# One more feed-forward tile by Strassen's scheme, and two small reorderings in the attention of a hybrid decoder block

## The chip, the cores and the metric

The kernel runs on one core of one Trainium2 chip. The metric is the device time of one execution, in microseconds (us). The engines are named as in the profile: PE multiplies matrices (PEld loads its weights), DVE and ACT work element by element, POOL and SP mostly issue transfers. Sixteen DMA engines move data.

## The reference, cut to what matters

One decoder layer on 512 tokens of width 1024. After an RMS norm, one projection feeds an attention mixer (8 heads; a compressed branch of 31 blocks, a selected and a sliding-window branch) and an RWKV-7 mixer. They are gated, merged and added to the residual. A second norm leads to the feed-forward part that most of the change is about:

```
def conv_ffn(h, w_up, conv_w, conv_b, w_down):
    u = h @ w_up
    s = u.shape[1]
    up = jnp.pad(u, ((0, 0), (CONV_WIDTH - 1, 0), (0, 0)))
    c = conv_b + conv_w[0] * up[:, 0:s]
    for j in range(1, CONV_WIDTH):
        c = c + conv_w[j] * up[:, j:j + s]
    val, gate = jnp.split(c, 2, axis=-1)
    return (jax.nn.silu(gate) * val) @ w_down
```

The other change is in the compressed branch of the attention:

```
    s_c = jnp.einsum('bgrsd,bcgd->bgrsc', q, kc).astype(jnp.float32) + bias_c
    p_c = masked_softmax(s_c, dist_c >= 0, axis=-1)
    o_cmp = jnp.einsum('bgrsc,bcgd->bsgrd', p_c, vc)
```

## The kernel before

Every large product is made of three products of 32-bit "rounded" parts: a weight tile is loaded by SP's queue into one of three `raw` buffers, ACT rounds it to `whi`, DVE subtracts to get `wlo` (L366), each with two buffers, and PE multiplies (hi, hi), (lo, hi) and (hi, lo). A load into a `raw` buffer is issued when DVE's split has read what was in it. `weight_tiles` lists all tiles in the order of use, `wload` issues a load, `wsplit` makes the parts, `wnext` hands out the next pair.

The order of the work on PE is written out by hand in the stretches named here (`manual_schedule`); the order on DVE and ACT there is a scheduler's. Four stretches matter, in order of time.

**Sums of weights in memory.** `sums_in_memory` makes, for the Strassen tiles, four sums of blocks of `w_up` in a memory array `usum` of 512 rows by 128 columns per Strassen tile. Sixteen copies and sixteen accumulating transfers, of 128 rows each, run on POOL's queue while the attention computes.

**Attention.** The loop over `units` (token tile, group, branches) takes two units at a time: `turns` transposes the weights `P` of a unit on PE (L1349), `scores` makes those of the unit two places later, `values` multiplies. Filler products (`filler`) with tiles of `w_proj_b` stand between. `compressed(qt)` is the softmax of the compressed branch for token tile `qt`: 8 products with `KC` on PE and some ten small steps on `sC`, mostly on DVE. Units 0 to 3 are token tile 3, units 4 to 7 tile 2, 8 and 9 tile 1, 10 and 11 tile 0. A unit's scores are left unscaled and their scalings (`pend`, one for a whole branch and four for rows) are run inside the next call of `scores`, spread over its groups (`ng` of them).

**Merge.** Eight tiles of `w_proj_a` (m = 0 to 7, 256 KB each), 12 products of 512 columns a tile, then `w_out`.

**Feed-forward.** 22 tiles of 128 features (f). A dense tile is 48 products of 512 columns, on two weight tiles of 512 KB. Tiles f in `SF` go by Strassen's scheme with 7 half products of 12 matmuls of 256 columns (L1613), on seven 256 KB halves, of blocks of `w_up` and of `usum`; two halves are one weight tile of the queue. Before them `up_tokens` (the generator `side`) makes sums of the activations in `Hw` and their parts `R1M2` and `R3Q`, some steps after each dense tile.

Of the kernel before, what the change touches and what calls it, by code (L numbers as in the profile page):

```python
# [22 lines left out]
KT = D // 128  # L23
DH = 64
H = 8
# [10 lines left out]
NGA = 1  # L36
NGB = 7
DECAY = math.exp(-0.5)
SF = range(4, 16)

O_Q, O_KC, O_VC, O_KS, O_VS, O_KW, O_VW, O_GATE, O_RWKV, O_GA, O_GB = (
    0, 512, 640, 768, 896, 1024, 1152, 1280, 1304, 3096, 4120)
# [42 lines left out]
def hybrid_block(ctx: ExitStack, tc: tile.TileContext, A: dict, out: bass.AP):  # L85
    nc = tc.nc
    v, sc, te = nc.vector, nc.scalar, nc.tensor
# [73 lines left out]
    for name in ("rwkv_mu", "rwkv_w0", "rwkv_a0", "rwkv_k_k", "rwkv_k_a", "rwkv_r_k", "rwkv_ln_g", "rwkv_ln_b"):  # L161
        r0, n = ROWS[name]
# [87 lines left out]
    def weight_tiles():  # L250
# [47 lines left out]
        stream = []  # L298
        for f in list(SF) + [None]:
# [8 lines left out]
                stream.append(up_block(p, 1, 1))  # L308
            if f is not None:
                stream += [up_sum(f, TS1), up_sum(f, TS3)]  # L310
        for i in range(0, len(stream) - 2, 2):
            yield stream[i:i + 2], KT, 128, v
        yield cols(A["w_up"][0], DFF + 128 * (SF[-1] + 1))
        yield stream[-2:], KT, 128, v
# [978 lines left out]
    def scores(u, n):  # L1293
        qt, g, bs = u
        qs = slice(128 * qt, 128 * qt + 128)
        N = 128 * (qt + 1)
        B = len(bs)
        P = Pb[units.index(u) % 4][:, 0:4 * B * N].rearrange("p (b r n) -> p b r n", b=B, n=N)
        nm = at.tile([128, 8], F32, name="nm", tag="nm", bufs=2)
        sm = at.tile([128, 8], F32, name="sm", tag="sm", bufs=2)  # L1300
        per = 512 // (B * N)
        todo, pend[:] = list(pend), []
        ng = 4 // per
        for r0 in range(0, 4, per):
            sp = pa()[:, 0:per * B * N].rearrange("p (r b n) -> p r b n", r=per, b=B)
            for r in range(r0, r0 + per):
                h = 4 * g + r
                for i, K in enumerate((KH, KL)):
                    mm(sp[:, r - r0], qst[:, h, qs], K[:, bs[0]:bs[0] + B, g, 0:N], i == 0, i == 1)
            for r in range(r0, r0 + per):  # L1310
                h = 4 * g + r
                for b in range(B):
                    i = 4 * b + r
                    v.tensor_tensor_reduce(out=P[:, b, r], in0=sp[:, r - r0, b], in1=BT[:, h, 384 - 128 * qt:512],  # L1314
                                           scale=-1.0, scalar=-NEG, op0=ALU.add, op1=ALU.min, accum_out=nm[:, i:i + 1])
                    act(P[:, b, r], P[:, b, r], AF.Exp, scale=-1.0, bias=nm[:, i:i + 1], accum_out=sm[:, i:i + 1])
            ig = r0 // per
            for f in todo[len(todo) * ig // ng:len(todo) * (ig + 1) // ng]:
                f()
            filler(n * (r0 + per) // 4 - n * r0 // 4)  # L1320
            yield
        v.reciprocal(sm[:, 0:4 * B], sm[:, 0:4 * B])
        for x, b in enumerate(bs):
            tt(sm[:, 4 * x:4 * x + 4], sm[:, 4 * x:4 * x + 4], gts[:, qt, 12 * g + 1 + b:12 * g + 12:3], ALU.mult)
        def row(b, r):
            i = 4 * b + r
            if r == 3:
                act(P[:, b, r], P[:, b, r], AF.Copy, scale=sm[:, i:i + 1])
            else:
                ts(P[:, b, r], P[:, b, r], sm[:, i:i + 1], None)  # L1330

        def branch(b):
            tt(P[:, b], P[:, b], sm[:, 4 * b:4 * b + 4, None].to_broadcast([128, 4, N]), ALU.mult)

        if B > 1:
            pend.append(lambda: branch(1))
        pend.extend(lambda r=r: row(0, r) for r in range(4))
        Ps[u] = P
# [50 lines left out]
    with tc.manual_schedule(engines=KTS):  # L1389
        run(scores(units[0], 12))  # L1390
        compressed(3)
        run(scores(units[1], 16))
        for i in range(0, len(units), 2):
            if i in (4, 8, 10):
                compressed_t(units[i][0])
            for j in (i, i + 1):
                a, b = turns(units[j]), scores(units[j + 2], nfill[j]) if j + 2 < len(units) else dense_only(nfill[j])
                alive = [a, b]
                while alive:
                    for x in list(alive):  # L1400
                        if next(x, alive) is alive:
                            alive.remove(x)
                    if j == 1 and len(PTk[units[1]]) == 2:
                        compressed_t(3)
            for j in (i, i + 1):
                values(units[j])
            for j in (i, i + 1):
                output(units[j])
            if i in (0, 4, 6):
                compressed({0: 2, 4: 1, 6: 0}[i])  # L1410
        filler(100)
    dbg("oaT", oaT.bitcast(F32))

# [185 lines left out]

    wpart = []  # L1600

    def up_weight():
        if not wpart:
            hi, lo = wnext(KT, 128)
            wpart.extend((hi[:, 4 * i:4 * i + 4], lo[:, 4 * i:4 * i + 4]) for i in range(2))
        return wpart.pop(0)

    def up_product(bank_, x, first=False):

        hi, lo = up_weight()  # L1610
        for k in range(8):
            for y in x[:2 - k // 4]:
                te.matmul(bank_, lhsT=(hi, lo)[k // 4][:, k % 4], rhs=y[:, k % 4], start=first and k == 0 and y is x[0],  # L1613
                          stop=k == 7, skip_group_check=not first)
# [14 lines left out]
    def up_strassen():  # L1629
# [4 lines left out]
        for f in list(SF) + [None]:  # L1634
            if f is not None:
                B1 = mmb()[:, b0]
                up_product(B1, H[0][0], True)
                u = [us[:, 3 * (f % 2) + k] for k in range(3)]
                Cg, Cv = craw[f % 2], craw[2 + f % 2]
                act(u[0], B1)  # L1640
                B2 = pa()[:, b0]
                up_product(B2, H[0][1], True)
                tt(Cg[:, b0], u[0], B2, ALU.add)
            else:
                following = dense_fm_g(hh, hl)
                next(following)
            if prev is not None:
                f_, B1_, B5_, u_, Cg_, Cv_ = prev
                up_product(B1_, H[1][1])
                act(Cg_[:, b1], B1_)  # L1650
                cg = conv(Cg_, NF + f_, f_ % 2)
            if f is not None:
                up_product(B1, M2)
                act(u[1], B1, AF.Copy, scale=-1.0)
            if prev is not None:
                up_product(B5_, Q)
                stt(Cv_[:, b0], B5_, -1.0, u_[1])
                cv = conv(Cv_, f_, 2 + f_ % 2)
                gate_value(f_, cg, cv)
            if f is not None:  # L1660
                B5 = pb()[:, b0]
                up_product(B5, R1, True)
                up_product(B1, R3)
                act(u[2], B1, AF.Copy, scale=-1.0)
                stt(Cv[:, b1], B5, -1.0, u[2])
                prev = f, B1, B5, u, Cg, Cv
# [3 lines left out]
    for f in range(NF):  # L1670
# [15 lines left out]
        if f // 2 < PD:  # L1686
            cv = conv(dense_fm(hh, hl) if f else lead[1], f, 2 + f % 2)
            gate_value(f, cg, cv)
            for _ in range(2):
                next(side, None)  # L1690
            continue
        act(cg, cg, AF.Silu)
# [232 lines left out]
```

## Time and profile before

| | |
|---|---|
| median of 3 runs | 803.11 us (802.75 to 803.26) |
| the profiled execution | 802.89 us |
| its span, first to last instruction | 801.1 us |
| outside the span | 1.8 us |
| granted clock of PE | 1.00 |
| PE, DVE, ACT, POOL busy | 790.1, 642.1, 482.8, 92.8 us |
| moved by DMA | 126.27 MB |

Times of places in the program are us from the start of the span of the profiled execution. Busy times of matmuls overlap one another, so the cost of one in a row of equal ones is read from the distance of their starts.

### The profile page before, as it was taken

To read this page: it belongs to the slowest core of one execution; us is meant where nothing else is said; L and a number is where in the kernel's file an instruction comes from. 1 tells how busy PE (TensorE), PEld (TensorE's weight loads), DVE (VectorE), ACT (ScalarE), POOL (GpSimd) and SP (SyncE) were. 2 spreads that over 40 slices of the span, in tenths; PEclk is the share of its full clock that TensorE was granted. 3 is DMA by queue.
4 is the path that set the end of the run, shared out by engine and by line. 5 is a ranking of instruction groups with operands and counts; after the bars stand their busy time and mean duration, and the time that the engine had idled before them with its cause. 6 is when DMAs were issued, how large, how long until landed. Compare 5 with 4: busy or idle time off the path is not lost.

```text
span 801.1 us, 14229 instructions
## 1 busy us (share of the span) xinstructions
PE 790.1 (99%) x5439; PEld 668.5 (83%) x5439; DVE 642.1 (80%) x1179; ACT 482.8 (60%) x929; POOL 92.8 (12%) x125
## 2 busy tenths in 40 slices
PE   7999999999999999999999999999999999999998
PEld 6788888887777887877788888999999888888886
DVE  4688899974565679888585489688898999989997
ACT  6777765454455678787344366677777754553452
POOL 5300021142000052221000000000000000002101
PEclk9999999999999999999999999999999999999999
DMA  7432323337362389999957134566666422584654
GB/s 221 125 90 68 99 74 105 86 101 210 80 132 54 79 227 271 261 261 269 196 183 243 50 133 118 154 185 182 173 184 182 128 79 80 181 309 167 234 179 153
DMA packets 138185, 126.27 MB, mean 158 GB/s; under 512 B 5806, under 2 KB 116069, under 8 KB 137989
## 3 DMA queue, kind: packets, MB, share of 16 engines
q1 hardware_dynamic: 123744, 83.21, 36.1%
q0 software_dynamic: 13312, 39.61, 18.5%
q10 hardware_dynamic: 1060, 2.55, 1.1%
q8 instruction: 42, 0.69, 0.4%
q14 instruction: 27, 0.21, 0.1%
HBM read 119.91 MB, written 29.56 MB: 187 GB/s over the span
## 4 chain that ended last, share of the span: by engine, by line
PE 90%; DVE 4%; DMA 4%; ACT 1%; issue 0%; POOL 0%; DVEq 0%
PE ps_mm L125 60%; PE ps_mm L1613 8%; PE ps_a L125 7%; PE ps_b L125 5%; PE ps_b L1613 4%; DMA usum<-in_w_up_dram 3%; PE ps_a L1613 2%; PE ps_b L1349 1%; DVE wlo L366 1%; PE ps_mm L1349 1%; DMA kc<-in_consts_dram 1%; DVE raw L131 0%; ACT whi L128 0%; PE ps_b L404 0%; PE ps_b L663 0%
## 5 line engine op out<-in xcount | busy, mean ns | idle before, releaser
L128 ACT ACTIVATE whi<-raw 128x1024 fp32r<-128x1024 f32 (+2 forms) x148 | 147.7, 999 | 129.9 <-PE ps_mm L125 61.0
L366 DVE TENSOR_TENSOR wlo<-raw,whi 128x1024 fp32r<-128x1024 f32 (+1 forms) x133 | 152.9, 1151 | 47.0 <-ACT whi L128 27.2
L125 PE MATMUL ps_mm<-hh,whi 128*128 128x512 f32 (+1 forms) x432 | 167.7, 391 | 0.3 <-ACT whi L128 0.2
L125 PE MATMUL ps_mm<-hl,whi 128*128 128x512 f32 (+1 forms) x432 | 160.5, 383 | 0.0
L125 PE MATMUL ps_mm<-hh,wlo 128*128 128x512 f32 (+1 forms) x432 | 107.9, 382 | 0.0
L125 PEld LDWEIGHTS ps_mm<-hh,whi 128*128 128x128 f32 x432 | 81.2, 188 | 18.4 <-issue 0.8
L125 PEld LDWEIGHTS ps_mm<-hh,wlo 128*128 128x128 f32 x432 | 81.2, 188 | 16.1 <-DVE wlo L366 0.3
L125 PEld LDWEIGHTS ps_mm<-hl,whi 128*128 128x128 f32 x432 | 79.2, 188 | 15.2 <-DVE hl L140 0.3
L1754 POOL DMA_DIRECT2D cgq<-in_w_down_dram x12 | 6.4, 535 | 290.0 <-DVE cgq L131 237.0
L128 ACT ACTIVATE P<-P,nm 128x512 f32<-128x512 f32 (+3 forms) x64 | 35.4, 555 | 4.5 <-DVE nm L1314 4.1
L131 DVE TENSOR_TENSOR cgq<-cgq 128x512 f32<-128x512 f32 (+1 forms) x49 | 32.9, 672 | 1.0 <-ACT cgq L128 0.2
L1314 DVE CUSTOM_DVE_ANT_0 P<-ps_a,AB 128x512 f32<-128x512 f32 (+3 forms) x64 | 30.1, 485 | 3.0 <-PE ps_a L125 2.9
L140 DVE SCALAR_TENSOR_TENSOR cgq<-cr,cw,cgq 128x511 f32<-128x511 f32 (+1 forms) x36 | 26.9, 748 | 4.4 <-ACT cgq L128 4.0
L140 DVE SCALAR_TENSOR_TENSOR cgq<-ps_mm,cw,cgq 128x511 f32<-128x511 f32 (+1 forms) x40 | 29.6, 746 | 1.1 <-ACT cgq L128 1.0
L1613 PE MATMUL ps_mm<-hl,whi 128*128 128x256 f32 x96 | 24.1, 283 | 0.0
L1613 PE MATMUL ps_mm<-hh,whi 128*128 128x256 f32 x96 | 24.1, 283 | 0.0
L128 ACT ACTIVATE QK<-ps_mm 128x64 f32<-128x64 f32 (+5 forms) x52 | 13.4, 303 | 15.3 <-PE ps_mm L125 15.2
L125 PE MATMUL ps_mm<-whi,hh 128*128 128x280 f32 (+2 forms) x72 | 22.4, 331 | 0.0
L128 ACT ACTIVATE ring<-cgq 128x1024 fp32r<-128x1024 f32 x12 | 12.7, 1060 | 15.8 <-DVE cgq L131 15.8
L125 PE MATMUL ps_mm<-whi,hl 128*128 128x280 f32 (+2 forms) x72 | 21.9, 323 | 0.0
L128 ACT ACTIVATE cgq<-ps_mm,cw 128x512 f32<-128x512 f32 x20 | 15.4, 776 | 8.8 <-PE ps_mm L125 8.0
L125 PE MATMUL ps_mm<-obT,whi 128*128 128x512 f32 x64 | 20.2, 397 | 0.0
(539 smaller groups left out, 1933.1 us busy)
## 6 DMA issues: line engine op xcount, KB each, us to landing
raw<-in_w_in_dram SPq DMA_DIRECT2D x38, 512.0 KB, 3.9
usum<-in_w_up_dram POOLq DMA_DIRECT2D x24, 768.0 KB, 23.6
raw<-in_w_down_dram SPq DMA_DIRECT2D x25, 512.0 KB, 4.0
raw<-usum SPq DMA_DIRECT2D x48, 256.0 KB, 3.3
raw<-in_w_up_dram SPq DMA_DIRECT2D x20, 512.0 KB, 3.8
raw<-in_w_up_dram SPq DMA_DIRECT2D x36, 256.0 KB, 3.3
usum<-usum POOLq DMA_DIRECT2D x8, 768.0 KB, 23.2
cgq<-in_w_down_dram POOLq DMA_DIRECT2D x12, 512.0 KB, 4.4
```

Source lines behind the costliest of these rows:

```text
L125: te.matmul(o, lhsT=l, rhs=r, start=start, stop=stop)
L128: sc.activation(o, i, f, **kw)
L131: v.tensor_tensor(o, a, b, op=op)
L140: v.scalar_tensor_tensor(o, a, s, b, op0=op0, op1=op1)
L366: eng.tensor_tensor(lo, raw, hi.bitcast(F32), op=ALU.subtract)
L1314: v.tensor_tensor_reduce(out=P[:, b, r], in0=sp[:, r - r0, b], in1=BT[:, h, 384 - 128 * qt:512], scale=-1.0, scalar=-NEG, op0=ALU.add, op1 ...
L1349: te.transpose(pt[:, 128 * i:128 * i + 128], P[:, x, i, 128 * k:128 * k + 128], ident)
L1613: te.matmul(bank_, lhsT=(hi, lo)[k // 4][:, k % 4], rhs=y[:, k % 4], start=first and k == 0 and y is x[0], stop=k == 7, skip_group_check=n ...
L1754: nc.gpsimd.dma_start(raws[g][i], A["w_down"][0][256 * g + 128 * i:256 * g + 128 * i + 128])
```

## The change

Three edits. Tile f = 3 joins the Strassen tiles, so there are 13 of them, f = 3 to 15, and three dense tiles ahead of them instead of four; `usum` grows from 1536 to 1664 columns. With 13 tiles the number of halves is odd, so the first half is a weight tile of its own, with four k-blocks. `side` takes three steps after each dense tile instead of two. In the attention, `compressed(0)` stands after the first unit of the fifth pair (j = 8) instead of after the fourth pair; and where `scores` has two groups (token tile 0), all five scalings are run after the first one.

```
-SF = range(4, 16)
+SF = range(3, 16)
...
-        for i in range(0, len(stream) - 2, 2):
+        yield stream[:1], 4, 128, v
+        for i in range(1, len(stream) - 2, 2):
             yield stream[i:i + 2], KT, 128, v
...
-            for f in todo[len(todo) * ig // ng:len(todo) * (ig + 1) // ng]:
+            for f in todo[len(todo) * ig // ng:len(todo) * (ig + 1) // ng] if ng > 2 else todo[5 * ig:5 * (ig + 1)]:
                 f()
...
+                if j == 8:
+                    compressed(0)
             for j in (i, i + 1):
                 values(units[j])
             for j in (i, i + 1):
                 output(units[j])
-            if i in (0, 4, 6):
-                compressed({0: 2, 4: 1, 6: 0}[i])
+            if i in (0, 4):
+                compressed({0: 2, 4: 1}[i])
...
-    def up_weight():
+    def up_weight(n=2):
         if not wpart:
-            hi, lo = wnext(KT, 128)
-            wpart.extend((hi[:, 4 * i:4 * i + 4], lo[:, 4 * i:4 * i + 4]) for i in range(2))
+            hi, lo = wnext(4 * n, 128)
+            wpart.extend((hi[:, 4 * i:4 * i + 4], lo[:, 4 * i:4 * i + 4]) for i in range(n))
         return wpart.pop(0)
...
-                up_product(B1, H[0][0], True)
+                up_product(B1, H[0][0], True, 1 if f == SF[0] else 2)
...
-            for _ in range(2):
+            for _ in range(3 if f < SF[0] else 2):
                 next(side, None)
```

On POOL, before, the end of the first run of sums (`usum` is the array of sums; a shape that splits a row of 128 is an accumulating transfer, the others are copies):

```order
L246 DMA usum<-in_w_up_dram 128x3x512
L243 DMA usum<-in_w_up_dram 128x1536
L246 DMA usum<-in_w_up_dram 128x3x512
L243 DMA usum<-in_w_up_dram 128x1536
L246 DMA usum<-usum 384x512
```

The same rows on POOL in the changed kernel:

```order
L246 DMA usum<-in_w_up_dram 128x4x416
L243 DMA usum<-in_w_up_dram 128x1664
L246 DMA usum<-in_w_up_dram 128x4x416
L243 DMA usum<-in_w_up_dram 128x1664
L246 DMA usum<-usum 416x512
```

The list keeps its order and its 32 transfers; each is wider by a twelfth, and those that add rows of `w_up` split a row into four pieces instead of three.

On DVE in the attention, before: the scaling of two rows of unit 9 (`P_3386`, last line) stands behind the softmax on `sC`, between the steps on the scores of unit 10 (`P_3387`).

```order
L131 TENSOR_TENSOR sC_3375<-sC_3375,kc 128x256
L366 TENSOR_TENSOR wlo<-raw,whi 128x512
L1279 TENSOR_REDUCE mx<-sC_3375 128x8
...
L1281 RECIPROCAL mx<-mx 128x8
L1314 ISA P_3387,nm<-ps_a,AB 128x128
L1314 ISA nm 128x1
L131 TENSOR_TENSOR mx<-mx,gts 128x8
L1314 ISA P_3387,nm<-ps_a,AB 128x128
L1314 ISA nm 128x1
L131 TENSOR_TENSOR sC_3375<-sC_3375,mx 128x256
L135 TENSOR_SCALAR P_3386<-P_3386,sm 128x256 x2
```

DVE at the same place in the changed kernel, from the two rows of unit 9 on:

```order
L135 TENSOR_SCALAR P_3386<-P_3386,sm 128x256 x2
L140 SCALAR_TENSOR_TENSOR AB<-AB,ps_mm 128x512
L367 TENSOR_TENSOR wlo<-raw,whi 128x512
L1315 ISA P_3387,nm<-ps_a,AB 128x128
...
L1260 COPY PTs<-ps_b 128x512
L131 TENSOR_TENSOR sC_3375<-ps_a,BC 128x256
```

The two rows are scaled ahead of the second group's scores, and the softmax begins only behind that group.

On DVE ahead of the Strassen tiles, before: `wlo_5225` and `wlo_5259` are the low parts of the last two weight tiles but two ahead of Strassen (the second of tile f = 2 and the first of f = 3), `R1M2` the low parts of summed activations.

```order
L140 SCALAR_TENSOR_TENSOR Hw_5127<-Hw_5127 128x1024
L131 TENSOR_TENSOR cgq_5120<-cgq_5120 128x512
L131 TENSOR_TENSOR R1M2_5123<-Hw_5127,R1M2_5123 128x1024
L131 TENSOR_TENSOR a2a_pairs_5128<-cgq_5120,a2a_pairs_5128 128x256
L366 TENSOR_TENSOR wlo_5225<-raw_5178,whi_5223 128x1024
L140 SCALAR_TENSOR_TENSOR cgq_5120<-ps_mm_5227,cw_72,cgq_5120 128x511
L366 TENSOR_TENSOR wlo_5259<-raw_5221,whi_5257 128x1024
```

The same place in the changed kernel: `wlo_5229` is the second weight tile of f = 2, `wlo_5264` the single half, `wlo_5310` the next two halves.

```order
L131 TENSOR_TENSOR R1M2_5123<-Hw_5127,R1M2_5123 128x1024
...
L131 TENSOR_TENSOR R1M2_5123<-Hw_5127,R1M2_5123 128x1024
L131 TENSOR_TENSOR cgq_5120<-cgq_5120 128x512
L131 TENSOR_TENSOR R3Q_5124<-Hw_5127,R3Q_5124 128x1024
L131 TENSOR_TENSOR a2a_pairs_5128<-cgq_5120,a2a_pairs_5128 128x256
L367 TENSOR_TENSOR wlo_5229<-raw_5180,whi_5227 128x1024
L140 SCALAR_TENSOR_TENSOR cgq_5120<-ps_mm_5231,cw_72,cgq_5120 128x511
L367 TENSOR_TENSOR wlo_5264<-raw_5225,whi_5262 128x512
L140 SCALAR_TENSOR_TENSOR cgq_5120<-ps_mm_5231,cw_72,cgq_5120 128x510
L131 TENSOR_TENSOR R3Q_5124<-Hw_5127,R3Q_5124 128x1024
L140 SCALAR_TENSOR_TENSOR cgq_5120<-ps_mm_5266,cw_72,cgq_5120 128x511
L367 TENSOR_TENSOR wlo_5310<-raw_5259,whi_5308 128x1024
```

Ahead of the second weight tile of f = 2 stand two more low parts of 1024 elements, one of `R1M2` and one of `R3Q`; ahead of the first whole Strassen weight tile stands the last `R3Q`.

## Rows read from the trace of the kernel before

**Rows 1.** The page, part 1: busy us (share of the span) of PE.

```profile
PE 790.1 (99%) x5439; PEld 668.5 (83%) x5439; DVE 642.1 (80%) x1179; ACT 482.8 (60%) x929; POOL 92.8 (12%) x125
```

**Rows 2.** Waits of PE: line waited for, us in total, times, longest.

```profile
PE ps_mm L1349 <- DVE P L135: 1.1, 1, 1.1
```

**Rows 3.** Windows: length, PE, PEld, DVE, ACT, POOL busy, clock, DMA share, GB/s.

```profile
482.50:493.40 10.90, 10.90 (x50) 9.03 (x49) 10.67 (x14) 7.14 (x11) 0.00 (x0) 1.00 0.32 94
```

**Rows 4.** The chain that ended last: start, us, engine, tile, line, instructions.

```profile
517.33 2.88 PE ps_b L1613 x24
...
628.64 77.76 PE ps_mm L125 x342
```

**Rows 5.** Timeline of PE in the attention: start, us, what, count, [idle before].

```profile
369.21 1.03 PE L1349 MATMUL ps_b<-kc,P 128*128 128x128 f32 x8
370.08 0.27 PE L1349 MATMUL ps_mm<-kc,P 128*128 128x128 f32 x1
371.47 0.70 PE L1349 MATMUL ps_mm<-kc,P 128*128 128x128 f32 x3 [1.12 <-DVE P L135]
371.93 0.36 PE L125 MATMUL ps_a<-KH,qst 128*128 128x256 f32 x1
```

**Rows 6.** Timeline of DVE in dense tiles f = 1 to 3.

```profile
483.47 0.75 DVE L140 SCALAR_TENSOR_TENSOR cgq<-ps_mm,cw,cgq 128x511 f32<-128x511 f32 x1 [0.23 <-ACT cgq L128]
...
489.14 1.22 DVE L366 TENSOR_TENSOR wlo<-raw,whi 128x1024 fp32r<-128x1024 f32 x1
490.27 0.74 DVE L140 SCALAR_TENSOR_TENSOR cgq<-ps_mm,cw,cgq 128x511 f32<-128x511 f32 x1
490.93 1.21 DVE L366 TENSOR_TENSOR wlo<-raw,whi 128x1024 fp32r<-128x1024 f32 x1
```

**Rows 7.** Timeline of PE at the end of tile f = 2.

```profile
491.52 1.98 PE L125 MATMUL ps_mm<-hh,wlo 128*128 128x512 f32 x8
```

**Rows 8.** Timeline of POOL: the first and the last sums.

```profile
286.28 2.11 POOL L243 DMA_DIRECT2D usum<-in_w_up_dram  x4
...
389.14 0.95 POOL L246 DMA_DIRECT2D usum<-usum  x1 [9.33 <-DMA usum<-usum]
```

**Rows 9.** DMA, 286:398: packets, MB, share; issues: KB each, median us to landing.

```profile
q0 software_dynamic: 8784, 25.30, 93.1%
...
raw<-in_w_proj_b_dram SPq DMA_DIRECT2D x7, 256.0 KB, 12.2
```

**Rows 10.** DMA, 380:385: packets, MB, share of 16 engines.

```profile
q0 software_dynamic: 423, 0.83, 89.7%
q1 hardware_dynamic: 428, 0.22, 21.6%
```

**Rows 11.** DMA issues near 389, 392, 394 and 401: last sum; w_proj_a m = 4, 5, 7.

```profile
usum<-usum POOLq DMA_DIRECT2D x1, 768.0 KB, 8.4
...
raw<-in_w_proj_a_dram SPq DMA_DIRECT2D x1, 256.0 KB, 6.0
...
raw<-in_w_proj_a_dram SPq DMA_DIRECT2D x1, 256.0 KB, 4.1
...
raw<-in_w_proj_a_dram SPq DMA_DIRECT2D x1, 256.0 KB, 2.6
```

**Rows 12.** Timeline of SP: issues of w_proj_a m = 4 and 5.

```profile
392.18 0.37 SPq L337 DMA_DIRECT2D raw<-in_w_proj_a_dram  x1
...
394.81 0.37 SPq L337 DMA_DIRECT2D raw<-in_w_proj_a_dram  x1
```

**Rows 13.** Timeline of ACT: high part of w_proj_a m = 4.

```profile
398.26 0.63 ACT L128 ACTIVATE whi<-raw 128x512 fp32r<-128x512 f32 x1 [1.98 <-DMA raw<-in_w_proj_a_dram]
```

**Rows 14.** Timeline of PE: first products of w_proj_a m = 4, 5, 6.

```profile
401.22 1.98 PE L125 MATMUL ps_mm<-oaT,whi 128*128 128x512 f32 x8
...
403.94 1.98 PE L125 MATMUL ps_mm<-oaT,whi 128*128 128x512 f32 x8
...
406.66 1.98 PE L125 MATMUL ps_mm<-oaT,whi 128*128 128x512 f32 x8
```

More of the change, by code (lines that the diff above doesn't have):

```diff
@@ L1600, in hybrid_block, with up_product @@
     wpart = []
-    def up_weight():
+    def up_weight(n=2):
         if not wpart:
-            hi, lo = wnext(KT, 128)
-            wpart.extend((hi[:, 4 * i:4 * i + 4], lo[:, 4 * i:4 * i + 4]) for i in range(2))
+            hi, lo = wnext(4 * n, 128)
+            wpart.extend((hi[:, 4 * i:4 * i + 4], lo[:, 4 * i:4 * i + 4]) for i in range(n))
         return wpart.pop(0)
-    def up_product(bank_, x, first=False):
-        hi, lo = up_weight()
+    def up_product(bank_, x, first=False, n=2):
+        hi, lo = up_weight(n)
         for k in range(8):
```

## The prediction, made before the changed kernel was run

> **What bounds the kernel now.** I read the busy times first: PE is busy 99% of the span [rows 1], so a gain must take work from PE or close one of its waits. The list of waits has little to close: apart from the start of the program, the one wait of note is 1.12 us at L1349, on a row scaling of DVE [rows 2, 5]. So I then went through the stretches that the change touches and asked how far PE's suppliers are from being late. In the dense tiles ahead of the Strassen tiles DVE is busy 10.67 of 10.90 us [rows 3]: whatever is put ahead of a weight split there makes it late. And from 286 to 398 us the sums in memory keep the DMA engines busy: POOL's queue q0 alone is 93.1% of 112 us [rows 9]. In that time a 256 KB weight tile lands 12.2 us after its issue [rows 9], against 2.6 us once the sums are over [rows 11]. The attention hides this. The merge, right behind it, takes a tile of w_proj_a every 2.72 us [rows 14], and the sums end just as it begins: the last one is issued at 389.14 and lands 8.4 us later, at 397.5 [rows 8, 11].
>
> **The tile that moves to Strassen.** A dense matmul of 512 columns costs 77.76/342 = 0.2274 us, a Strassen one of 256 columns 2.88/24 = 0.120 us [rows 4]. Dense tile: 48 x 0.2274 = 10.92. Strassen tile: 7 x 12 x 0.120 = 10.08. PE saves **0.84 us**. From the second Strassen tile on the halves pair up as before, so the steady state of that stretch should not change.
>
> **DVE ahead of the Strassen tiles.** The low part of the second weight tile of f = 2 starts at 489.14 before. The new order puts two more low parts of 1024 elements ahead of it; one such step takes 490.27 - 489.14 = 1.13 us of DVE. An idle 0.23 us at 483.47 is used up [rows 6]. So it starts at 489.14 + 2.26 - 0.23 = 491.17 and ends 1.22 us later, at 492.39. PE asks for it at 491.52 [rows 7]: **0.87 us** late. Behind it come a conv step (490.93 - 490.27 = 0.66 us [rows 6]), the half split (half of 1.13, say 0.60), a conv step, the last low part of R3Q (1.13) and a conv step: 3.71 us after 492.30, the first whole Strassen weight tile is started at 496.01 and ready at 497.23. PE, 0.87 us late, ends f = 2 eight products of 0.2274 us after 492.39, at 494.21; then come one half product (1.44) and the hi products of the next (0.96), so it asks at 496.61: another **0.62 us**. Together **1.5 us**, more than the tile saves. The rows show no spare time of DVE but the 0.23 us already used; the bounds are 0 (DVE in time after all, rival 2) and 2.2, one more conv step of 0.66 late.
>
> **The attention.** Eight transposes take 370.08 - 369.21 = 0.87 us, so the four at 370.08 need 0.43; the next group starts at 371.93 [rows 5]. The loss is 1.85 - 0.43 = 1.42 us. In the changed kernel the two row scalings stand ahead of the second group's scores, and the eight products of the softmax move to just before the transposes on PE, which costs nothing and gives DVE more time. The softmax's result is needed only by the last pair of units. Queued behind it on DVE are the scores of unit 11, which that last pair uses too, so a pair of units lies between. I take the whole **1.42 us**; the bounds are 0 and 1.42.
>
> **The sums in memory.** All 32 transfers grow by 13/12. q0's work was 0.931 x 112 = 104 us [rows 9], so by bytes it grows by 8.7 us, and since the queue is backlogged the last sum lands at about 406.2 instead of 397.5. If instead every packet costs the same whatever its size, the eight transfers cut into four pieces add 8 x 128 packets and the eight wider sums 8 x 32, at 104/8784 us each: 15 us, plus 2 for the copies (2048 packets, a twelfth longer): 17. If all of it went into gaps: 0. I take 8.7, because copies and sums kept the engines above nine tenths busy the whole time.
>
> What hides it now is that the merge starts when the sums end. In 380 to 385 us the two queues alternate packet by packet, 423 to 428, and the weights get 0.22 MB in 5 us [rows 10], so a 256 KB tile takes 6.0 us of the queue. Tile m = 4 was issued at 392.18 and landed 6.0 us later; m = 5 at 394.81, 4.1 us later, 1.4 us behind the last sum [rows 11, 12]. ACT waited 1.98 us for m = 4 and PE did not [rows 13, 14]: 398.26 + 0.63 = 398.89, against 401.22. That slack of 2.3 us is all there is.
>
> In the changed kernel the attention ends 1.42 us earlier, so m = 4 is issued at about 390.8 and m = 5 at 393.4, both well inside the sums. m = 4 lands between 396.8 (as before) and 403.0 (12.2 us); I take 401.7, near the upper end, since the sums run on, but go singly at the end and leave gaps. m = 5 stands behind it in the same queue: 6.0 us more, 407.7, or 1.4 us behind the last sum, 407.6; with the gaps, 406.0. ACT splits it by 406.65 and PE starts it then, instead of at 403.94: **2.7 us later than before**, the attention's gain already eaten. PE then reaches m = 6 at 409.4; that tile lands in the 2.6 us behind m = 5, so nothing is added. Bounds for m = 5: no stall at all (PE at 403.94 - 1.42 = 402.5) and, with sums that end 17 us later, the limit passes to m = 6: 6.0 us behind an m = 5 at 407.7, 413.7, split by 414.35 instead of 406.66, 7.7 us later.
>
> Here a page of the notes gives another answer. The Trainium skill, page "DMA: Bandwidth & Descriptors", section "Anatomy of one DMA", fits a DMA (of POOL's path) by 2.0 us plus its bytes over 436 GB/s, an estimate of 2.6 us for 256 KB. The row of m = 7 has just that; the rows under the sums have 12.2. If the page's time held under load there would be no stall and the sum would be 802.1; the rows decide.
>
> **The sum.** 802.89 (the profiled execution; span 801.1 and 1.8 around it) + 2.7 at m = 5, the attention's gain included + 1.5 on DVE - 0.84 = **806.3**. The profiled execution is 0.2 under the median of the runs shown, which is within their spread. A measurement of this kernel can tell about 0.2%, 1.6 us.
>
> **The rivals.**
> 1. *The longer sums stay hidden.* The weight tiles of the merge land in time, and the three other terms are left: -1.42 + 1.5 - 0.84 = -0.8, **802.1**, not slower. For it: PE did not wait for m = 4 before, although ACT did. Against it: the slack of 2.3 us and the 12.2 us of a load. It decides when m = 5 lands by 402.5 - 0.65 = 401.8, that is, if the last sum lands by about 400.4, 2.9 us later than before. Chance 0.20; the skill's fit above would make it sure.
> 2. *Hidden sums, and DVE in time.* If the split of f = 2 is ready at 491.52, only the two gains count: -2.3, **800.6**. The DVE rows leave no idle time for that. Chance 0.09.
> 3. *Packets, not bytes.* The narrower accumulating packets cost as much as the wide ones, the sums end 17 us later and m = 6 is held too: 802.89 + 7.7 + 1.5 - 0.84 = **811.3**. Chance 0.15.
> 4. *The attention's wait comes back elsewhere,* for instance as unit 11's scores waiting for the softmax. Ahead of the merge this changes little: a PE that comes 1.42 us later meets the same landing of m = 5. It ends within my forecast's own range.
>
> **How the numbers follow.** The forecast has 0.56; its own range is 804.5 to 808.5 (the sums' end 2 us earlier or later, DVE's stall 0.5 to 2.2), of which a little falls within 0.2%. Slower by over 0.2% (above 804.7): 0.52 of the forecast and 0.15 of rival 3, 0.67. Within 0.2%: rival 1 and the rest of the forecast, 0.24. Faster (below 801.5): 0.09. The range 801.6 to 810.0 leaves out rival 2 and about half of rival 3.
>
> **What would show it.** Right: in the profile after, no wait of PE at L1349; the last sum issued near 397 and landed near 406; ACT waits for raw<-in_w_proj_a, and PE waits at the first products of m = 4 or 5, 3 to 5 us in all; m = 4 and 5 landing some 11 and 12 us after their issue; two waits of PE on wlo L367 near the first Strassen tile, 0.9 and 0.6 us. The forecast is wrong if w_proj_a still lands within 6 us of its issue, if the sums' last landing hardly moves, or if DVE runs its splits earlier than the order of its rows allows.

## The result, and the profile after

The changed kernel takes 809.31 us (median of 6 executions, 808.79 to 811.99) against 802.95 (802.59 to 803.26): the ratio of the means is 1.0084, 95% interval 1.0071 to 1.0098. It is slower by 6.4 us. The forecast was 806.3, 3.4 us slower: the sign was right, the size half of what came. The profiled execution took 809.23 us, its span 807.4.

The page, part 1, of the changed kernel; PE's share, 99% in [rows 1], is 98% now:

```profile
PE 792.5 (98%) x5475; PEld 671.4 (83%) x5475; DVE 644.3 (80%) x1184; ACT 484.6 (60%) x935; POOL 92.8 (11%) x125
```

Waits of PE in the changed kernel (total, times, longest). The wait at the row scalings of [rows 2] is gone. These are the largest that came in its place:

```profile
PE ps_mm L125 <- ACT whi L128: 2.8, 2, 2.6
PE ps_a L1616 <- DVE wlo L367: 1.4, 1, 1.4
PE ps_mm L1616 <- ACT us L128: 0.6, 1, 0.6
```

A wait of 0.4 us at the start of the program (for DVE's `h`) is new too; it lies far ahead of what was changed and comes and goes between the profiles (0.8 in a_attn, none in e_wide).

**Where the time goes.** The starts of `w_out`, of dense tile f = 1 and of the down products cut the program in pieces. PE's timeline of the kernel before, from the start of the merge:

```profile
390.29 2.23 PE L125 MATMUL ps_mm<-oaT,whi 128*128 128x512 f32 x9
...
412.10 0.39 PE L125 MATMUL ps_mm<-whi,mTh 128*128 128x512 f32 x1
...
471.44 0.50 PE L125 MATMUL ps_mm<-hh,whi 128*128 128x512 f32 x1 [0.20 <-ACT whi L128]
...
691.28 0.61 PE L125 MATMUL ps_mm<-whi,a2a_pairs 128*128 128x512 f32 x2
```

PE's timeline of the changed kernel, with the merge (m = 4 at 402.24, m = 5 at 407.53, m = 6 at 410.73) and the first Strassen tile:

```profile
388.54 2.23 PE L125 MATMUL ps_mm<-oaT,whi 128*128 128x512 f32 x9
...
402.24 3.78 PE L125 MATMUL ps_mm<-oaT,whi 128*128 128x512 f32 x8 [2.62 <-ACT whi L128]
...
407.53 2.44 PE L125 MATMUL ps_mm<-oaT,whi 128*128 128x512 f32 x8
...
410.73 1.98 PE L125 MATMUL ps_mm<-oaT,whi 128*128 128x512 f32 x8
...
416.17 0.39 PE L125 MATMUL ps_mm<-whi,mTh 128*128 128x512 f32 x1
...
417.85 0.50 PE L125 MATMUL ps_mm<-whi,mTh 128*128 128x512 f32 x1 [0.16 <-DVE ta L140]
...
475.96 0.50 PE L125 MATMUL ps_mm<-hh,whi 128*128 128x512 f32 x1 [0.21 <-ACT whi L128]
...
496.09 0.28 PE L1616 MATMUL ps_mm<-hh,whi 128*128 128x256 f32 x1
...
497.04 2.00 PE L125 MATMUL ps_mm<-hh,wlo 128*128 128x512 f32 x8
...
499.35 0.28 PE L1616 MATMUL ps_a<-hh,whi 128*128 128x256 f32 x1
...
501.83 0.74 PE L1616 MATMUL ps_a<-hh,wlo 128*128 128x256 f32 x4 [1.36 <-DVE wlo L367]
502.40 1.12 PE L1616 MATMUL ps_mm<-R1M,whi 128*128 128x256 f32 x8
...
506.07 1.22 PE L1616 MATMUL ps_mm<-R3Q,whi 128*128 128x256 f32 x8 [0.63 <-ACT us L128]
...
697.56 0.62 PE L125 MATMUL ps_mm<-whi,a2a_pairs 128*128 128x512 f32 x2
```

Up to the start of `w_out` 4.07 us are lost, to f = 1 another 0.45, to the down products 1.76, together 6.28. The merge and the first Strassen tile are the two places. Eight matmuls that took 1.98 us in [rows 14] take 3.78 at 402.24: the windows say why (length; PE, PEld, DVE, ACT, POOL busy; granted clock; DMA share; GB/s):

```profile
400.00:402.00 2.00, 0.00 (x0) 0.00 (x0) 0.00 (x0) 0.45 (x1) 0.00 (x0) 0.90 1.13 267
402.00:404.00 2.00, 1.76 (x4) 1.48 (x5) 1.26 (x3) 0.70 (x2) 0.00 (x0) 0.50 1.13 218
404.00:406.00 2.00, 2.00 (x6) 1.52 (x6) 1.78 (x4) 1.15 (x2) 0.00 (x0) 0.50 1.02 194
406.00:408.00 2.00, 2.00 (x7) 1.52 (x6) 1.58 (x4) 0.00 (x0) 0.00 (x0) 0.50 0.52 133
...
410.00:412.00 2.00, 2.00 (x10) 1.64 (x9) 2.00 (x4) 1.26 (x2) 0.00 (x0) 1.00 0.18 68
```

PE did nothing from 400 to 402, and behind that wait its granted clock is 0.50, the 1.2 GHz level, for 6 us. The timeline of ACT shows when the weights were there (the high parts of m = 4, 5 and 6; the step starts when the load has landed):

```profile
401.56 0.63 ACT L128 ACTIVATE whi<-raw 128x512 fp32r<-128x512 f32 x1 [6.14 <-DMA raw<-in_w_proj_a_dram]
...
404.27 0.63 ACT L128 ACTIVATE whi<-raw 128x512 fp32r<-128x512 f32 x1 [1.56 <-DMA raw<-in_w_proj_a_dram]
...
408.77 0.63 ACT L128 ACTIVATE whi<-raw 128x512 fp32r<-128x512 f32 x1 [3.35 <-DMA raw<-in_w_proj_a_dram]
```

The timelines of SP and POOL have the issues of m = 6 and of the last sum, and the DMA view (KB, us to landing) the same two:

```profile
397.41 0.37 SPq L338 DMA_DIRECT2D raw<-in_w_proj_a_dram  x1
...
398.45 0.96 POOL L246 DMA_DIRECT2D usum<-usum  x1 [10.99 <-DMA usum<-usum]
```

```profile
raw<-in_w_proj_a_dram SPq DMA_DIRECT2D x1, 256.0 KB, 11.3
...
usum<-usum POOLq DMA_DIRECT2D x1, 832.0 KB, 10.0
```

The last sum lands at 408.4, 10.9 us later than in [rows 8, 11], and m = 6 at 408.7, right behind it. Each of these three loads took about 11 us from its own issue (11.0, 11.1 and 11.3).

### The profile page after: what moved, and what is told of

It is laid out like the page before. It is cut to its first block, busy times and chain, and to the rows that moved or that the text cites. A ratio compares the mean times of both kernels' runs of the same rounds, so it can differ in the third digit from the quotient of the medians.

```text
span 807.4 us, 14326 instructions
## 1 busy us (share of the span) xinstructions
PE 792.5 (98%) x5475; PEld 671.4 (83%) x5475; DVE 644.3 (80%) x1184; ACT 484.6 (60%) x935; POOL 92.8 (11%) x125
## 5 line engine op out<-in xcount | busy, mean ns | idle before, releaser
L125 PE MATMUL ps_mm<-hh,whi 128*128 128x512 f32 (+1 forms) x416 | 161.5, 391 | 0.3 <-ACT whi L128 0.2
L125 PE MATMUL ps_mm<-hl,whi 128*128 128x512 f32 (+1 forms) x416 | 154.3, 383 | 0.0
L125 PE MATMUL ps_mm<-hh,wlo 128*128 128x512 f32 (+1 forms) x416 | 104.0, 382 | 0.0
L125 PEld LDWEIGHTS ps_mm<-hh,whi 128*128 128x128 f32 x416 | 78.2, 188 | 17.7 <-issue 0.8
L125 PEld LDWEIGHTS ps_mm<-hh,wlo 128*128 128x128 f32 x416 | 78.1, 188 | 15.5 <-DVE wlo L367 0.3
L125 PEld LDWEIGHTS ps_mm<-hl,whi 128*128 128x128 f32 x416 | 76.2, 188 | 14.6 <-DVE hl L140 0.3
L140 DVE SCALAR_TENSOR_TENSOR cgq<-ps_mm,cw,cgq 128x511 f32<-128x511 f32 (+1 forms) x36 | 26.6, 745 | 0.8 <-ACT cgq L128 0.8
L1616 PE MATMUL ps_mm<-hl,whi 128*128 128x256 f32 x104 | 26.1, 283 | 0.0
L1616 PE MATMUL ps_mm<-hh,whi 128*128 128x256 f32 x104 | 26.1, 283 | 0.0
L125 PE MATMUL ps_mm<-oaT,whi 128*128 128x512 f32 x64 | 18.1, 430 | 2.6 <-ACT whi L128 2.6
```

What stands on the lines that cost most here:

```text
L125: te.matmul(o, lhsT=l, rhs=r, start=start, stop=stop)
L140: v.scalar_tensor_tensor(o, a, s, b, op0=op0, op1=op1)
```

## The experiments

Each time is a median, compared with the kernel before on the same chip (medians of 802.86 to 802.95 there); the ratio is that of the means.

| run | what it is | us | ratio to before, 95% interval |
|---|---|---|---|
| a_attn | attention edits alone | 801.42 | 0.9982 (0.9973 to 0.9991) |
| k_comp | later softmax alone | 801.85 | 0.9983 (0.9975 to 0.9992) |
| k_scal | scalings in one group alone | 802.20 | 0.9986 (0.9978 to 0.9995) |
| c_noattn | changed, without attention edits | 810.85 | 1.0089 (1.0075 to 1.0103) |
| b_sums12 | changed, sums as wide as before, the 13th tile's left out | 803.75 | 1.0014 (1.0003 to 1.0024) |
| i_pieces | before, sums in four pieces | 802.84 | 1.0001 (0.9992 to 1.0010) |
| d_warm | changed, PE kept busy in the wait | 808.33 | 1.0065 (1.0052 to 1.0077) |
| e_wide | changed, w_proj_a in wider tiles, issued earlier | 802.40 | 0.9997 (0.9988 to 1.0006) |
| f_late | changed, Q's parts later | 808.12 | 1.0063 (1.0050 to 1.0075) |
| g_widelate | e_wide and f_late | 801.48 | 0.9982 (0.9973 to 0.9991) |
| j_best | g_widelate, R3's parts later too | 800.87 | 0.9969 (0.9958 to 0.9981) |
| h_attnwide | a_attn and wider tiles, 12 Strassen tiles | 801.47 | 0.9978 (0.9968 to 0.9987) |

### The merge: is it the sums, the loads or the clock?

Sums of the old width, in the changed kernel:

```
-    usum = dp.tile([4, 512, 128 * len(SF)], F32, name="usum")
+    usum = dp.tile([4, 512, 128 * (len(SF) - 1)], F32, name="usum")
...
-        o = 128 * (f - SF[0])
+        o = 128 * min(f - SF[0], len(SF) - 2)
...
-        return A["w_up"][0][512 * i + 128 * k:512 * i + 128 * k + 128, o:o + 128 * len(SF)]
+        return A["w_up"][0][512 * i + 128 * k:512 * i + 128 * k + 128, o:o + 128 * (len(SF) - 1)]
```

> The changed kernel with the sums in memory as wide as before, 12 tiles; the thirteenth Strassen tile reads the sums of the twelfth (its own are left out). Theory A (the merge is late because the sums end 9 us later): no wait of PE at w_proj_a, no fall of the granted clock, the merge starts w_out 1.75 us before its old time of 412.1; 809.3 - 4.07 - 0.43 - 1.75 = 803.1 us. Rival (the loads of w_proj_a are late because the attention asks for them earlier, not because of the longer sums): about 809 us with the wait at m=4.

803.75 us: without the thirteenth tile's columns in the sums 5.6 us come back. The rival, about 809 us, is out. The median is 0.6 above Theory A. The profiled execution, at 805.52 the second slowest of eleven, shows what can be left: its last sum landed at 402.6, and PE still waited for m = 5 (at a granted clock of 1.00):

```profile
403.59 2.11 PE L125 MATMUL ps_mm<-oaT,whi 128*128 128x512 f32 x8 [1.42 <-ACT whi L128]
```

So the sums' end moves from profile to profile: in six with sums of 12 tiles (before, a_attn, b_sums12, i_pieces, k_comp, k_scal) the last one lands at 397.5, 400.0, 402.6, 399.3, 399.4 and 400.2. With 13 tiles (changed, c_noattn, d_warm, f_late) it is 408.4, 409.2, 409.5 and 408.2. The means are 9.0 us apart; by bytes I had 8.7. (The kernels with wider loads below are left out here.)

More packets for the same bytes, in the kernel before:

```
-                                    accum_op=ALU.add, max_dma_last_dim=2048)
+                                    accum_op=ALU.add, max_dma_last_dim=1536 if type(src) is tuple else 2048)
```

> The kernel before, 12 tiles wide in the sums, with the accumulating transfers that read the weights cut into four pieces a row instead of three: the same bytes in 8 x 128 more packets. Bytes decide: the last sum lands at 397.5 as before, 802.9 us. Packets decide: 1024 x 104/8784 = 12.1 us later, near 409.6, PE waits at m=4 to m=6 as in the changed kernel without the attention edits, 806 to 809 us. In between (the last sum came 10.9 us later in the changed kernel, where bytes alone give 8.7): a wider row costs most of it, 2 us here, last sum at 399.5, 802.9 to 804 us.

802.84 us, and the last sum at 399.3, inside the spread of 12-tile sums: the 1024 additional packets cost nothing that can be seen. Rival 3 of the prediction falls; bytes decide.

The attention as before, in the changed kernel:

```
-                if j == 8:
-                    compressed(0)
...
-            if i in (0, 4):
-                compressed({0: 2, 4: 1}[i])
+            if i in (0, 4, 6):
+                compressed({0: 2, 4: 1, 6: 0}[i])
...
-            for f in todo[len(todo) * ig // ng:len(todo) * (ig + 1) // ng] if ng > 2 else todo[5 * ig:5 * (ig + 1)]:
+            for f in todo[len(todo) * ig // ng:len(todo) * (ig + 1) // ng]:
```

> The changed kernel without the attention edits: 13 Strassen tiles and wider sums alone. PE comes to the merge 1.75 us later than in the changed kernel; m=4 to m=6 land as there. Theory A (the landing of m=6, ready at 409.4, bounds the merge, and the clock's fall hides in front of it): PE waits 1.0 us at m=4, the clock need not fall, then 1.7 us more at m=6; w_out starts at 414.9, 808.0 us, 809.3 if the clock falls all the same. Theory B (the wait is short and the clock's fall is the rest): with a wait of 1.0 us the clock stays up and the merge loses nothing more, 806.3 us. Theory C (the attention's gain is kept in the changed kernel): 811.1 us.

810.85 us, nearest to Theory C; but the interval takes in Theory A's 809.3 and the changed kernel as well, so five executions don't decide. The profile goes against what both A and B took for granted. I had let the loads land where they landed in the changed kernel; m = 4, 5 and 6 were issued 1.4 to 1.6 us later with the later attention, were there for ACT 0.9 to 3.5 us later, and the clock fell too, behind a second wait (rows of PE, then windows, as above):

```profile
403.18 2.11 PE L125 MATMUL ps_mm<-oaT,whi 128*128 128x512 f32 x8 [1.96 <-ACT whi L128]
...
408.42 3.57 PE L125 MATMUL ps_mm<-oaT,whi 128*128 128x512 f32 x8 [1.59 <-ACT whi L128]
```

```profile
404.00:406.00 2.00, 1.65 (x8) 1.05 (x7) 2.00 (x4) 0.00 (x0) 0.00 (x0) 1.00 1.09 201
...
410.00:412.00 2.00, 2.00 (x6) 1.56 (x5) 2.00 (x5) 1.02 (x2) 0.00 (x0) 0.50 0.19 10
```

`w_out` starts at 418.33, 2.2 us behind the changed kernel's. So it is likely, but not shown, that the attention's gain reaches the end even through a merge that waits, because the loads start with it.

PE kept busy in the wait, in the changed kernel:

```
+        if m == 4:
+            dummy = pa()
+            for i in range(11):
+                mm(dummy, oaT[:, 0, 0, 0:128], oaT[:, 0, 0], True, True)
         pA = dense_fm(oaT[:, 0], oaT[:, 1], 4)
```

> The changed kernel with 11 products of 512 columns on data at hand, whose result nobody reads, ahead of m=4 (2.5 us of PE in the wait of 2.62 us). The clock should stay at full. Theory A (m=6 lands no earlier): PE runs m=4 and m=5 at full clock and then waits 1.7 us for m=6, whose high part is ready at 409.4; w_out at 414.9 instead of 416.2, 808.0 us. Theory B (the half clock costs its 3.05 us in full): 806.3 us. If the products only push m=4 back by their own time: 811 to 812 us.

808.33 us, Theory A to 0.3 us. PE's timeline and the windows:

```profile
399.28 2.65 PE L125 MATMUL ps_a<-oaT 128*128 128x512 f32 x11
401.91 2.14 PE L125 MATMUL ps_mm<-oaT,whi 128*128 128x512 f32 x8
...
410.55 2.11 PE L125 MATMUL ps_mm<-oaT,whi 128*128 128x512 f32 x8 [1.40 <-ACT whi L128]
...
416.13 0.39 PE L125 MATMUL ps_mm<-whi,mTh 128*128 128x512 f32 x1
```

```profile
404.00:406.00 2.00, 1.68 (x7) 1.14 (x7) 0.91 (x3) 1.15 (x2) 0.00 (x0) 1.00 1.12 211
```

The clock stays at 1.00, PE is through with m = 5 earlier, and then it waits for m = 6, which here landed at 409.8, 1.1 us later than in the changed kernel; `w_out` starts at the same time. The half clock adds 3.05 us to m = 4 and 5 in the changed kernel (8.49 us from 402.24 to 410.73, against 5.44 in [rows 14]). That the kernel loses all of it (Theory B, 806.3) is out; the run without it gives back 1.0 in the medians, with intervals that still overlap, and nothing at `w_out` in the two profiles. The rest would have been spent waiting for m = 6: at full clock PE would have come to it at 402.24 + 5.44 = 407.68, before its weights at 409.40.

Wider tiles of `w_proj_a`, in the changed kernel: four loads of 512 KB with rows of 1 KB, each used for two m. They take the places of the first four loads in the queue, so the last of them goes out far earlier than m = 6 did:

```
-        for m in range(KT):
-            yield cols(A["w_proj_a"][0], 128 * m, NH2)
+        yield from ((A["w_proj_a"][0][:, o:o + 256], NH2, 256, v) for o in range(0, D, 256))
...
-        pA = dense_fm(oaT[:, 0], oaT[:, 1], 4)
+        if m % 2 == 0:
+            wa = wnext(NH2, 256)
+        pA = mmb()
+        for i in range(2):
+            for k in range(NH2):
+                for y in range(2 - i):
+                    mm(pA, wa[i][:, k, 128 * (m % 2):128 * (m % 2) + 128], oaT[:, y, k], i + k + y == 0, i == 1 and k == NH2 - 1)
```

> The changed kernel with w_proj_a loaded as four tiles of 256 columns (rows of 1 KB in memory instead of 512 bytes, as many packets for twice the bytes; three buffers then hold six m instead of three). Everything else, the sums too, is as in the changed kernel. Theory A (the merge is late because its loads share the queue with sums that end at 408): the last pair, m=6 and 7, is issued near 383.5 and lands within some 17 us, by 400.5, before PE asks at 404.9; no wait of PE, no fall of the clock, w_out at 410.3; 809.3 - 4.07 - 0.43 - 1.75 = 803.1 us. Rival (a 512 KB load under the sums takes twice the 11 us of one of 256 KB): the last pair lands at 405.5 or later, a wait of 1 to 2 us stays, 804 to 807 us.

802.40 us: 6.9 us come back, although the Strassen start still waits as in the changed kernel (1.4 us for DVE's wlo). PE's timeline (m = 6, `w_out`); SP's issue of the last load; and, from the DMA view, the last sum and the second load:

```profile
404.70 1.98 PE L125 MATMUL ps_mm<-oaT,whi 128*128 128x512 f32 x8
...
410.14 0.39 PE L125 MATMUL ps_mm<-whi,mTh 128*128 128x512 f32 x1
```

```profile
383.79 0.37 SPq L337 DMA_DIRECT2D raw<-in_w_proj_a_dram  x1
```

```profile
usum<-usum POOLq DMA_DIRECT2D x1, 832.0 KB, 11.0
...
raw<-in_w_proj_a_dram SPq DMA_DIRECT2D x1, 512.0 KB, 12.2
```

PE waits for no load, and its granted clock is 1.00 all through the merge, although the last sum, issued at 400.61, lands at 411.6. That settles the merge: late loads are its whole loss, the clock's fall included. What made them timely is not taken apart: the rows are wider, and the load with m = 6 and 7 goes out at 383.79, where m = 6 went out at 397.41. No run here has one without the other.

### The first Strassen tile

The seventh step of the activation sums (Q's parts) inside the first Strassen tile:

```
-            assert next(side, 0) == 0
             a2b = pairs(fp, "a2b", 6, (2,))
...
                 act(u[1], B1, AF.Copy, scale=-1.0)
+                if prev is None:
+                    assert next(side, 0) == 0
...
-            for _ in range(3 if f < SF[0] else 2):
+            for _ in range(2):
```

> The changed kernel with two steps of the activation sums after each dense tile instead of three, the seventh (the parts of Q) inside the first Strassen tile; nothing else moved. The parts of Q need 1.1 us of DVE, which then no longer stand ahead of the low part of the first whole Strassen weight tile. Theory A (PE waits there because DVE is a step late): the wait of 1.36 us shrinks to 0.3 or less and the wait for ACT's us behind it goes too; 809.3 - 2.3 = 807.0 us. Rival (the stall only moves, to Q's parts at the end of the first tile, or the merge's wait takes the gain): 808.5 to 809.5 us.

808.12 us: 1.2 us gained of the 2.3 that I expected, between Theory A and the rival. From f = 1 to the down products the profile is 1.4 us shorter. The wait is shorter, not gone, since R3's low part still stands ahead of the split on DVE:

```profile
500.75 0.74 PE L1616 MATMUL ps_a<-hh,wlo 128*128 128x256 f32 x4 [0.50 <-DVE wlo L367]
```

With the wider tiles as well (the diffs of e_wide and f_late together):

> Both cures on the changed kernel: w_proj_a in four tiles of 256 columns, and the parts of Q inside the first Strassen tile. If the two stalls are all that ate the gains, 809.3 - 6.25 - 2.3 = 800.8 us, below the kernel before and the two attention edits alone (801.4). If they overlap or something else waits: 802 to 804 us.

801.48 us, 0.7 above what I expected, with the same 0.5 us wait. So R3's parts were moved too, behind the second half:

```
                 tt(Cg[:, b0], u[0], B2, ALU.add)
+                if prev is None:
+                    next(side)
...
-            for _ in range(2):
+            for _ in range(2 if f < SF[0] - 1 else 1):
```

> As g_widelate, and the parts of R3 as well as those of Q are made inside the first Strassen tile (five steps of the activation sums on the dense tiles). In g_widelate a wait of 0.5 us on DVE's wlo of the first whole Strassen weight tile was left, with one more low part (1.1 us of DVE) ahead of that wlo. Theory A: that wait goes, and nothing takes its place, since R3 is wanted some 5 us later: 801.48 - 0.6 = 800.9 us, 0.5 below the kernel with the attention edits and wide loads alone, where the tile's arithmetic gives 0.84. Rival: R3's parts come too late and PE waits there: 801.5 to 802 us.

800.87 us, as expected, and the lowest median of the study: 0.9969 of the kernel before. The wait of f_late and g_widelate is gone; a smaller one shows at a later half:

```profile
500.05 0.75 PE L1621 MATMUL ps_mm<-hh,wlo 128*128 128x256 f32 x4 [0.34 <-DVE wlo L366]
```

Its control, with 12 tiles: the two attention edits and the wider loads, put into the kernel before:

> The control for the thirteenth tile: the kernel before (12 Strassen tiles, sums as before) with the two attention edits and the wide loads of w_proj_a. With 12 tiles the loads were in time by 0.6 us in the profile, late in some executions; the wide loads should only take away the late ones: 801.3 us with the highest executions below 802. Against j_best this is what the thirteenth tile is worth without its stalls: 0.84 us by arithmetic, nothing if it still meets a wait.

801.47 us, highest 801.96. The thirteenth tile is worth 0.6 us by the medians, though the intervals of the two kernels overlap, and 0.25 at the start of the down products of the two profiled executions. The arithmetic gave 0.84. The wait that j_best has there accounts for the difference in the profiles: by the distance of starts it costs 0.6 us (from 499.43 to 500.63 five starts take 1.20 us, where they take 0.60 without a wait).

### The attention alone

Both edits, on 12 tiles (in the kernel before, the lines that c_noattn undoes):

> The kernel before with the two attention edits alone (12 Strassen tiles, sums as before). Theory A (the merge waits only where a weight tile lands late): PE comes to the merge 1.75 us earlier and asks for m=4 at 399.5, where its high part was ready at 398.9 before, so nothing waits and the whole 1.75 us is kept: 801.2 us. Rival (the margin of 0.6 us is too small, or the loads, issued earlier into the sums, land later): PE waits at m=4 or m=5, the gain is lost there, 802.5 to 803.5 us.

801.42 us, Theory A: 1.5 us kept. Its two highest executions, near 802.7, fit the rival. PE starts `w_out` 1.97 us earlier than before (410.13) and f = 1 only 1.40 earlier (470.04): 0.57 us go between, at a wait for DVE's `ta`:

```profile
411.96 0.50 PE L125 MATMUL ps_mm<-whi,mTh 128*128 128x512 f32 x1 [0.31 <-DVE ta L140]
```

The later softmax alone:

```
+                if j == 8:
+                    compressed(0)
...
-            if i in (0, 4, 6):
-                compressed({0: 2, 4: 1, 6: 0}[i])
+            if i in (0, 4):
+                compressed({0: 2, 4: 1}[i])
```

> The kernel before with the later softmax of token tile 0 alone, the scalings spread over the two groups as before. On DVE the whole softmax is then behind the scores of unit 10, and the two scalings of unit 9 follow those scores with nothing of the softmax between. Theory A (the softmax steps ahead of the scalings made PE wait): 1.1 us or more of the 1.5 that both edits gained, 801.5 to 801.8 us. Theory B (the scalings' place behind the second group of scores is the cause): no gain, 802.9 us, the wait of 1.1 us at the transposes stays.

The scalings alone:

```
-            for f in todo[len(todo) * ig // ng:len(todo) * (ig + 1) // ng]:
+            for f in todo[len(todo) * ig // ng:len(todo) * (ig + 1) // ng] if ng > 2 else todo[5 * ig:5 * (ig + 1)]:
```

> The kernel before with all scalings of units 8 and 9 after the first group of the next scores, the softmax of token tile 0 where it was. On DVE the two scalings of unit 9 come ahead of the last steps of the softmax and of the second group of scores. Theory A (the softmax decides): 0.5 us of the gain or less, 802.4 to 802.9 us. Theory B (the scalings' place decides): the wait at the transposes goes, 801.5 to 801.8 us, if the second group of scores, now behind them, makes nothing late.

801.85 and 802.20 us: the first just above its Theory A, the second between its two theories. Each takes the wait at the transposes away in its profile, and the merge starts at 388.58 and 388.72, against 390.29 before. So neither place alone is the cause: it is enough that softmax and scalings no longer stand one behind the other ahead of the transposes. That the later softmax gains more than the moved scalings is inside the spread.

## Why the prediction was right or wrong

| term | predicted | measured |
|---|---|---|
| merge, attention's gain included | +2.7 | +4.07 |
| `w_out` to f = 1 | none | +0.45 |
| DVE ahead of Strassen | +1.5 | +2.6 |
| tile saving | -0.84 | -0.84 taken as predicted (0.25 between the profiles of j_best and h_attnwide, with a wait of 0.6 left) |
| sum | +3.4 | +6.3 |

**The attention: right in the main.** The wait is gone; the merge starts 1.75 us earlier (388.54 against 390.29), 1.42 predicted, 1.5 in the medians. Of rival 4 a part came: in a_attn 0.57 us go again behind the merge, at DVE's `ta`.

**The sums: right by bytes, wrong in their start.** They grew by 9.0 us, not by 17 (rival 3) and not by 2.9 or less (rivals 1 and 2). I added the growth to one landing, 397.5, the earliest of the six shown since, and so had the end at 406.2 where it came at 408.4.

**The merge: right mechanism, the wait right by luck, and the step that failed.** I had m = 5 need 6.0 us of the queue behind m = 4, hold PE until 406.65, and PE go on from there at full pace. m = 4 landed where I had it (401.4, 401.7 predicted), but m = 5 landed at 404.2 and not at 406.0: the loads overlap, each some 11 us behind its own issue. It was m = 6, issued at 397.41, still among the sums, that came last. Its high part was ready at 408.77 + 0.63 = 409.40, just where I had PE arrive by way of a late m = 5. So the wait for data comes to the 2.7 us predicted, by another tile and from sums that ended 2.2 us later than I took: two errors that cancel, which is luck.

The step that failed is "so nothing is added" behind m = 5. The sum has PE come to m = 6 at 409.4 and then run on; PE came at 410.73, 1.33 us after the weights, because m = 4 and 5 ran at half the clock behind the first wait, a cost that I had put at nothing. 409.40 - 406.66 [rows 14] + 1.33 = 4.07.

How much of the time is the clock's beyond this one execution stays open. In the profiles of d_warm and f_late the clock stays at 1.00, and `w_out` still starts 4.03 and 3.46 us later than before: PE waits there 0.3 to 0.4 us at a time for low parts of these tiles from DVE, and in d_warm m = 6 landed 1.1 us later. Of the six executions of the changed kernel one had a mean granted clock of 1.000 and took 809.22 us; the profiled one had 0.996 and took 809.23. So 3.5 to 4.1 us go in the merge with the clock's fall or without it, and what is shown is that they come from the late loads (b_sums12, e_wide).

The Trainium skill, page "TensorE: Matmul & The Clock Gate", section "HAM oscillation — how this bites in real kernels", tells of such a loop, where waits for transfers bring the clock down, and prices it as half of the throttled time: 3 us here, as an estimate for the 6 us at 0.50. The fall behind the wait agrees with the trace, and so does the price for PE's own work, 3.05 us in m = 4 and 5; of the kernel's time it is 1.33 us at most in this profile, since m = 6 would have held PE for the rest.

**Behind the merge: a term that the sum lacks.** The 0.45 us between `w_out` and f = 1 go at 417.85, where PE waits for DVE's `ta`. DVE's timeline of the changed kernel has it ready just then:

```profile
417.11 0.68 DVE L140 SCALAR_TENSOR_TENSOR ta<-sg,ps_mm 128x512 f32<-128x512 f32 x1
```

DVE works there without a gap from 409.96 on, behind the late m = 6, and has not caught up. The same stretch is 0.57 to 0.91 us longer than before in a_attn, b_sums12, d_warm and f_late, 0.1 to 0.4 longer in i_pieces, k_comp and k_scal, and not longer in c_noattn (0.02) nor with the wider loads (59.29 to 59.32 us, 59.34 before). So it seems to hang on when the tiles come; how, is not shown.

**DVE ahead of Strassen: right place, mis-sized.** DVE was as late as I had it: f = 1 starts 4.52 us later now, which puts my two splits at 496.91 and 501.75; they were ready at 496.86 and 501.77. What I had wrong is when PE asks. The first wait (0.87) did not show: PE's order has the eight high products of the half (496.09) ahead of the low products that need it (497.04). I read DVE's order and not PE's. The second wait (0.62) is 1.36. DVE's timeline has the low part of R3Q ahead of the split, as the order said:

```profile
495.64 1.22 DVE L367 TENSOR_TENSOR wlo<-raw,whi 128x1024 fp32r<-128x1024 f32 x1
...
498.70 1.21 DVE L131 TENSOR_TENSOR R3Q<-Hw,R3Q 128x1024 fp32r<-128x1024 f32 x1
499.89 0.75 DVE L140 SCALAR_TENSOR_TENSOR cgq<-ps_mm,cw,cgq 128x511 f32<-128x511 f32 x1
500.56 1.21 DVE L367 TENSOR_TENSOR wlo<-raw,whi 128x1024 fp32r<-128x1024 f32 x1
```

Because PE lost nothing at the first place, it came to the second earlier; 1.36 is near the 1.49 of both. What the term lacks is a third wait behind them, 0.63 us for ACT's copy `us`, which I had not seen: it stands on ACT behind a `whi` that waits for PE (by the row; most likely to free a buffer):

```profile
504.08 1.06 ACT L128 ACTIVATE whi<-raw 128x1024 fp32r<-128x1024 f32 x1 [2.23 <-PE ps_mm L1616]
...
505.66 0.36 ACT L128 ACTIVATE us<-ps_mm 128x256 f32<-128x256 f32 x1
```

From f = 1 to the down products 1.76 us are lost with the tile's 0.84 gained, so the stalls cost 2.6, 0.6 more than the two waits. The distance of starts has nearly all of it: from 499.35 to 502.40 a half product takes 3.05 us instead of 1.44, so the wait of 1.36 costs 1.61, and the one of 0.63 likewise costs 0.9. That the first comes from DVE's order is shown by f_late and j_best, where it shrinks with each low part that is moved: 1.36, 0.50, none. The one for `us` goes with it (0.63, 0.17, none), but is also smaller without any such edit: 0.2 to 0.4 in c_noattn, d_warm, b_sums12 and e_wide.

## What to carry to other kernels

When a long background transfer ends close to a stage that consumes loads one by one, check every load issued before that end, not only the first late one, and take the end's spread over executions into the range. A DVE-bound lead-in must be read in the orders of all engines: PE's order hid one late split, ACT's queue added a wait of its own. Where loads share the DMA engines with a bulk transfer, ask for the same bytes in fewer, wider loads, so that the last goes out earlier: that took the sums off the path here, with the sums no shorter.

## What was not expected of the hardware

- Under the sums a 512 KB load in rows of 1 KB took 12.2 us to land, the 256 KB load in rows of 512 bytes that the changed kernel issues at the same place took 10.8. Twice the bytes came nearly free, and the sums seem to have paid: their last landing is 411.6 to 413.1 in the three profiles with 13 tiles and wide loads, 408.2 to 409.5 in the four without. This fits the alternation by packets in [rows 10]; the Trainium skill, "DMA: Bandwidth & Descriptors", section "Queues, rings and completion order", has each engine take turns between its queues a packet at a time.
- The same bytes in 1024 more packets on POOL's queue cost nothing that can be seen (i_pieces, 802.84 us against 802.86).
- The granted clock fell to 0.50, the 1.2 GHz level, behind one wait of 2.62 us in the changed kernel; in f_late it stayed at 1.00 behind one of 2.03 us; in c_noattn it was 1.00 behind a wait of 1.96 us and 0.50 behind another of 1.59 us, five microseconds later.
